# Asking for the modulation's weight blocks four steps ahead, from the point where a group's heads begin

## The chip, the core and the metric

The kernel runs on one core of a Trainium2 chip. The metric is the device time of one execution in microseconds (us); below 0.3% two times of this kernel are taken as no different. TensorE (PE, with its weight loads listed apart as PEld), VectorE (DVE), ScalarE (ACT) and GpSimd (POOL) each run their own instructions in order; almost all transfers between memory and the on-chip buffers are asked for on the queue of SyncE (SP), which also is worked off in order.

## The reference

One layer of a hybrid encoder, for a prompt of 2048 tokens and a sample of 64, width 1024. The part that matters is the modulation, six vectors that depend on the conditioning vectors alone:

```
mod = (c_act @ w_ada + b_ada)[:, None, :]
sh1, sc1, gt1, sh2, sc2, gt2 = jnp.split(mod, 6, -1)
h = rmsnorm(x, g1) * (1 + sc1) + sh1
proj = h @ w_in                                  # pool columns, q, k, v, o, gates
...
mix = jnp.concatenate([pool_out, hs], -1) @ w_out
x = x + gt1 * mix
h2 = rmsnorm(x, g2) * (1 + sc2) + sh2
up = h2 @ w_up
...
x = x + gt2 * ((jax.nn.silu(g) * a) @ w_down)
```

`c_act` has two rows, one for the prompt and one for the sample. `w_ada` is 1024 x 6144 in float32. `sh2`, `sc2` and `gt2` are first needed behind the attention part.

## The kernel before

**Two stages.** The attention stage (input projection, mLSTM heads, pooling, output projection) takes the tokens in four groups of 512, the last with the 64 sample tokens besides. Then the feed-forward stage takes them in three groups of 704. In the trace the attention stage lies between 0 and about 760 us. All matrix products are made of three passes of a high and a low half of each operand; so weights are either split on the chip (ACT makes the high half, L411, DVE the low half, L414) or read back in a form split before.

**One group of the attention stage.** The loop over `groups` (from L1450) first makes the v columns and the gates (`proj_v`, PE at L1133), then for each of four heads three projections (`gemm`, PE at L478) with the mLSTM steps of the head before woven in (`lstm`: the transposes of k at L1298, q by k at L1308, the state update `kw` by `va` at L1323, the read-out at L1343 and L1345), then pooling and the output projection. `lstm`'s vector instructions are recorded by a helper and all stand at L250 in the trace: `kw` is the scaled, transposed k that L1323 needs.

**Work in the background.** Generators lie in the lists `bg`; `tick(i)` moves the first generator of list i one step on. In the second to fourth groups list 3 holds `ada(2 + o.g, False)`, which makes one of `sh2`, `sc2`, `gt2`, and list 4 holds `up_sums` (L852 to L882), which reads `w_up` in pieces into `w4` tiles (L857), forms sums on DVE (L876 to L881) and stores them as `wsum` (L867). Both share SP and DVE with the weights and the mLSTM steps.

**`ada` (L177).** A modulation vector's weights are 16 blocks of 128 x 512 float32, 256 KB each. `load(i)` asks for block i on SP (L194). Step i takes block i and makes two DVE instructions, one for each conditioning row: at L208 for the first block of a half (a product), at L210 for the others (product and sum). In the second to fourth groups `lead` is 3: the first tick asks for blocks 0, 1 and 2, and step i ends with asking for block i + 3.

**Where its ticks are.** In `proj_v` list 3 is ticked for the second product (`hv == 0`) at even token tiles: four times in the second and third groups, six times in the fourth, which has a fifth tile. So the heads begin with step 3, in the fourth group with step 5. After that each `gemm` ticks list 3 twice, once at its fifth weight block and once at its end (L487, L492).

**The tiles.** The blocks lie in `raw` tiles, of which there are five (`RB`, L44). The same five tiles hold the weights that are split on the chip: `w_v` for `proj_v`, and `w_out` for the output projection. The head projections of the second to fourth groups read `hl_kept`, already split, into the seven `wt` tiles (L395) and use no `raw` tile.

**What sets the order.** Only the first group's opening and the feed-forward stage have their instruction order written out by hand (`manual_schedule`, L1457 and L2004). In the rest of the attention stage the framework orders each engine's instructions, SP's requests among them, from the order in which they are written, their dependencies, priorities and free tiles. An instruction can thus stand well ahead of where it is written. Once ordered, the order is fixed, and each engine waits where it must.

## Time and profile before

| | |
|---|---|
| median of 3 runs | 2174.8 us |
| lowest and highest run | 2169.42 us, 2175.45 us |
| the profiled execution's own time | 2174.68 us |
| its span, first to last instruction | 2172.9 us |
| lying around the span | 1.8 us |
| mean granted TensorE clock | 0.998 of full speed |
| requests for blocks of `ada` on SP in the second to fourth groups | 48, of 256 KB each |
| from such a request to its landing, min / median / max | 3.0 / 5.4 / 6.8 us |

The page gives each engine's busy time in the whole span. The views of waits name the instruction that waited, then the one it waited for, then the total in us, the number of times and the longest. The chain of waits follows the work that ended last back to its releasers. A timeline row has start, duration, engine, line, operation and operands, a count, and in brackets the engine's idle time before it with the releaser. A window's row has its length, the busy time of PE, PEld, DVE, ACT and POOL with instruction counts, the granted clock, the DMA share and GB/s.

### The profile page before, as it was taken

How to read it: one execution, taken by the hardware profiler on the slowest of the kernel's cores; microseconds unless marked ns; L12 is line 12 of the kernel's file. 1: busy time of each engine (PE TensorE's matmuls, PEld its weight loads, DVE VectorE, ACT ScalarE, POOL GpSimd, SP SyncE). 2: the span in 40 equal slices, each digit the busy share in tenths (PEclk: the TensorE clock that was granted, in tenths of full speed). 3: DMA queues.
4: the chain of work that ended last, by engine and by line, in shares of the span. 5: the costliest groups of instructions: out<-in, count | busy, mean ns of one | idle time of the engine just before them, and what ended most of it. 6: DMA issues, size and time to landing. Idle time of an engine off the chain costs nothing.

```text
span 2172.9 us, 38060 instructions
## 1 busy us (share of the span) xinstructions
PE 2151.4 (99%) x13553; PEld 2044.4 (94%) x13553; DVE 1634.9 (75%) x3040; ACT 1096.1 (50%) x2181; POOL 258.4 (12%) x475
## 2 busy tenths in 40 slices
PE   8999999999999999999999999999999999999998
PEld 7888888888899999999999999999999999999998
DVE  5878668667955778797967668888886597887874
ACT  4554335334333446464736445655655365565554
POOL 0010000001000201010101220100101321111112
PEclk9999999999999999999999999999999999999999
DMA  8987997987888477888967976666668675555542
GB/s 319 328 305 233 323 321 246 309 302 244 301 283 288 169 260 239 282 292 300 350 214 255 321 245 222 234 208 209 228 222 274 223 255 186 170 177 190 171 160 77
DMA packets 297351, 539.51 MB, mean 248 GB/s; under 512 B 25760, under 2 KB 114336, under 8 KB 297160
## 3 DMA queue, kind: packets, MB, share of 16 engines
q1 hardware_dynamic: 286568, 511.87, 69.6%
q10 hardware_dynamic: 10592, 25.20, 3.0%
q8 instruction: 107, 1.75, 0.3%
q14 instruction: 84, 0.69, 0.1%
HBM read 410.98 MB, written 125.98 MB: 247 GB/s over the span
## 4 chain that ended last, share of the span: by engine, by line
PE 85%; DMA 5%; DVE 5%; issue 2%; ACT 2%; SPq 0%; POOL 0%; DVEq 0%; ACTq 0%; POOLq 0%
PE mm L1594 34%; PE mm L478 22%; PE mm L2160 12%; PE mm L2037 8%; PE mm L1133 3%; DVE wt L414 1%; DMA wt<-wsum 1%; PE m L1323 1%; DMA hl_kept<-wt 1%; PE m L1308 1%; PE m L1343 1%; PE m L1345 1%; DVE tg L1572 1%; DMA raw<-w_qkou 0%; ACT wt L411 0%
## 5 line engine op out<-in xcount | busy, mean ns | idle before, releaser
L1594 PE MATMUL mm<-hx,wt 128*128 128x352 f32 x5544 | 885.9, 321 | 0.7 <-DVE wt L414 0.5
L1594 PEld LDWEIGHTS mm<-hx,wt 128*128 128x128 f32 x5544 | 878.7, 188 | 2.6 <-DVE wt L414 2.0
L478 PE MATMUL mm<-hl,wt 128*128 128x512 f32 (+2 forms) x1920 | 387.4, 357 | 0.0
L411 ACT ACTIVATE wt<-raw 128x512 fp32r<-128x512 f32 (+3 forms) x470 | 276.6, 597 | 177.6 <-PE mm L478 52.8
L478 PEld LDWEIGHTS mm<-hl,wt 128*128 128x128 f32 x1920 | 316.4, 189 | 47.7 <-issue 4.4
L414 DVE TENSOR_TENSOR wt<-raw,wt 128x512 fp32r<-128x512 f32 (+3 forms) x470 | 312.8, 672 | 61.9 <-ACT wt L411 61.7
L2160 PE MATMUL mm<-av,wt 128*128 128x448 f32 (+1 forms) x1632 | 262.7, 322 | 0.0
L2160 PEld LDWEIGHTS mm<-av,wt 128*128 128x128 f32 x1632 | 250.4, 188 | 11.1
L2009 DVE SCALAR_TENSOR_TENSOR x<-mm,MOD,x 128x352 f32<-128x352 f32 (+3 forms) x360 | 167.5, 505 | 77.7 <-PE mm L2160 64.3
L2037 PE MATMUL mm<-av,wt 128*128 128x352 f32 x1344 | 220.7, 323 | 1.9 <-DVE x L2009 0.7
L2037 PEld LDWEIGHTS mm<-av,wt 128*128 128x128 f32 x1344 | 215.4, 188 | 5.0 <-DVE ea L1603 3.0
L1641 ACT ACTIVATE mm<-mm 128x352 f32<-128x352 f32 x196 | 87.8, 448 | 233.7 <-PE mm L1594 177.1
L478 PE MATMUL mm<-mx,wt 128*128 128x512 f32 (+1 forms) x960 | 182.9, 352 | 0.3 <-DVE scr L250 0.3
L478 PEld LDWEIGHTS mm<-mx,wt 128*128 128x128 f32 x960 | 159.4, 188 | 23.0 <-PE mm L478 0.5
L1572 DVE SCALAR_TENSOR_TENSOR ta<-ea,V,ta 128x704 f32<-128x704 f32 (+1 forms) x132 | 125.7, 953 | 58.4 <-ACT ta L1567 54.4
L1572 DVE SCALAR_TENSOR_TENSOR tg<-eg,V,tg 128x704 f32<-128x704 f32 (+1 forms) x132 | 125.7, 952 | 56.8 <-ACT tg L1567 54.3
L414 DVE TENSOR_TENSOR wt<-wt 128x512 fp32r<-128x512 f32 x196 | 133.0, 685 | 12.8 <-ACT wt L411 12.7
L411 ACT ACTIVATE wt<-wt 128x512 fp32r<-128x512 f32 x196 | 119.2, 622 | 36.6 <-DMA wt<-wsum 35.7
L1550 POOL COPY ea<-UC 128x2 f32<-128x2 f32 x66 | 33.1, 501 | 506.2 <-DVE ta L1572 407.3
L1781 ACT ACTIVATE tg<-tg 128x704 f32<-128x704 f32 (+1 forms) x66 | 52.5, 795 | 71.8 <-DVE tg L1572 71.8
L1133 PE MATMUL mm<-wt,hl 128*128 128x256 f32 (+1 forms) x576 | 71.4, 284 | 0.0
L1133 PEld LDWEIGHTS mm<-wt,hl 128*128 128x128 f32 x576 | 70.4, 190 | 0.8 <-issue 0.6
(305 smaller groups left out, 2207.0 us busy)
## 6 DMA issues: line engine op xcount, KB each, us to landing
wt<-wsplit SPq DMA_DIRECT2D x132, 512.0 KB, 4.3
raw<-w_up SPq DMA_DIRECT2D x198, 256.0 KB, 3.8
wt<-hl_kept SPq DMA_DIRECT2D x96, 512.0 KB, 6.3
wt<-wsum SPq DMA_DIRECT2D x132, 256.0 KB, 5.0
wsplit<-wt SPq DMA_DIRECT2D x66, 512.0 KB, 5.1
w<-w_up SPq DMA_DIRECT2D x88, 256.0 KB, 4.4
wsum<-w SPq DMA_DIRECT2D x44, 512.0 KB, 5.9
Bd<-fscr ACTq DMA_DIRECT2D x56, 352.0 KB, 4.3
```

The source lines that it names most:

```text
L411: act.activation(u.w[:, 0, :u.n], u.raw[:, :u.n], AF.Copy)
L414: dve.tensor_tensor(out=u.w[:, 1, :u.n], in0=u.raw[:, :u.n], in1=u.w[:, 0, :u.n].bitcast(F32), op=ALU.subtract)
L478: pe.matmul(ps[bi][:, :hi - lo], U[:, a, k % 4 * P:(k % 4 + 1) * P], mv[k][:, b, lo:hi], start=(at == 0 and pi == 0), stop=(k == order[-1] ...
L1133: pe.matmul(ps[ti][:n, :cols], h[4 * kh + k4][:, b, lo:lo + n], U[:, a, k4 % 2 * cols:(k4 % 2 + 1) * cols], start=(kh == 0 and k4 == 0 and ...
L1550: pool.tensor_copy(ext[:, 0:2], UC[:, f, :])
L1572: dve.scalar_tensor_tensor(out=t[:, :E], in0=ext[:, j:j + E], scalar=wc(j, f), in1=t[:, :E], op0=ALU.mult, op1=ALU.add)
L1594: pe.matmul(bk.t[:, :FH], U[:, a, kc * P:(kc + 1) * P], Bo.at(nm, kc, b), start=(first and kc == 0 and pi == 0), stop=(kc == 3 and pi == 2 ...
L1641: act.activation(to.t[:, :FH], bk.t[:, :FH], AF.Copy)
L1781: act.activation(self.tg[:, :E], self.tg[:, :E], AF.Silu)
L2009: dve.scalar_tensor_tensor(out=x3[n][:, a:b], in0=bk.t[:, a - lo:b - lo], scalar=gt2(n, s), in1=x3[n][:, a:b], op0=ALU.mult, op1=ALU.add)
L2037: pe.matmul(bk.t[:, :FH], U[:, a, c:c + P], quad.put(op, m, b), start=(first and m == 0 and pi == 0), stop=(m == 1 and pi == 2), skip_grou ...
L2160: pe.matmul(bks[i].t[:, :hi - lo], U[:, a, k % 4 * P:(k % 4 + 1) * P], av[k][:, b, lo:hi], start=(k == 0 and (a, b) == PASSES[0]), stop=(k ...
```

## The change

A list `ahead_of_heads` is empty while `proj_v` of the second, third or fourth group is written, and holds an entry from then on. When `ada` ends a step while it holds one and `lead` is still 3, `lead` becomes 4 and one more block is asked for. From there step i asks for block i + 4. No instruction is added: blocks 7 to 15 of the second and third groups and blocks 9 to 15 of the fourth are each asked for one step earlier than before. The first group's `ada` has a `lead` of 4 in both kernels and other tiles, and isn't touched.

```diff
+    ahead_of_heads = []
+
     def ada(m, first):
...
             load(i + lead)
+            if ahead_of_heads and lead == 3:
+                lead = 4
+                load(i + lead)
             yield
         side.append(ada_end(m, accs))
...
             else:
                 cols = []
+                ahead_of_heads.clear()
                 va = proj_v(o, h, cols)
+                ahead_of_heads.append(1)
```

## The prediction

> **What bounds the kernel now.** I read the page's busy times first.

> ```profile
> span 2172.9 us, 38060 instructions
> ...
> PE 2151.4 (99%) x13553; PEld 2044.4 (94%) x13553; DVE 1634.9 (75%) x3040; ACT 1096.1 (50%) x2181; POOL 258.4 (12%) x475
> ```

> PE is idle for 2172.9 - 2151.4 = 21.5 us of the whole span. So I went to the stretches in which the change can act, the four heads of the second, third and fourth groups, in the view by windows (length, then PE's busy time):

> ```profile
> 237.00:347.00 110.00, 110.00 (x581) 92.48 (x581) 77.53 (x173) 40.16 (x113) 9.48 (x13) 1.00 0.84 286
> 415.00:529.00 114.00, 112.15 (x585) 93.89 (x583) 74.67 (x171) 40.65 (x114) 10.21 (x14) 0.99 0.82 279
> 604.00:720.00 116.00, 115.13 (x855) 109.36 (x854) 63.80 (x178) 42.53 (x134) 8.20 (x11) 1.00 0.80 262
> ```

> PE has no gap in the second group, 1.85 us in the third and 0.87 us in the fourth. That is the whole idle time to be won in the place of the change. The view of PE's waits from 405 to 530 us has a single row, which names the third group's gap:

> ```profile
> PE m L1323 <- DVE kw L250: 1.9, 1, 1.9
> ```

> The chain of waits over the same place says why `kw` was late (start, duration, what):

> ```profile
> 427.53 0.63 SPq L194
> ...
> 428.20 5.81 DMA raw<-w_ada
> ```

> A block of `ada`, asked for at 427.53, is 5.81 us on its way; DVE, which works in order, had its update queued ahead of `kw` (DVE's rows stand below), and PE waited for `kw`. This is the event that the change can touch.

> It costs more than its gap. Here is the same run of 39 matmuls, from the first head's L1285 to its read-out, in the second and in the third group, and then the window just behind the gap:

> ```profile
> 255.90:261.80 5.90, 5.90 (x39) 5.17 (x37) 4.28 (x10) 1.14 (x4) 0.00 (x0) 1.00 1.07 392
> 433.70:443.50 9.80, 7.95 (x39) 6.59 (x39) 9.51 (x22) 1.14 (x4) 0.00 (x0) 0.83 0.92 347
> ```

> ```profile
> 438.50:441.90 3.40, 3.40 (x12) 2.94 (x12) 3.29 (x9) 0.00 (x0) 0.00 (x0) 0.50 1.06 407
> ```

> The granted clock is 0.50 for 3.4 us right behind the gap. The PE timeline gives the price exactly:

> ```profile
> 255.75 0.39 PE L1285 MATMUL m<-RHL,E_r 128*128 128x512 f32 x1
> ...
> 261.67 0.39 PE L1343 MATMUL m<-SP,q 128*128 128x129 f32 x2
> ```

> ```profile
> 433.76 0.39 PE L1285 MATMUL m<-RHL,E_r 128*128 128x512 f32 x1
> ...
> 435.24 0.94 PE L478 MATMUL mm<-hl,wt 128*128 128x512 f32 x3
> 438.03 1.65 PE L1323 MATMUL m<-va,kw 128*128 128x129 f32 x8 [1.85 <-DVE kw L250]
> ...
> 443.37 0.38 PE L1343 MATMUL m<-SP,q 128*128 128x129 f32 x2
> ```

> From L1285 to L1343 the second group takes 261.67 - 255.75 = 5.92 us, the third 443.37 - 433.76 = 9.61 us: 3.69 us more, of which 1.85 us is the gap and 1.84 us the slower matmuls (half of 3.4 us would be 1.7 us).

> [...]

> **The change part by part.** *Requests.* None is added and none removed; 9 + 9 + 7 = 25 of the 48 move forward by one step, each past what SP has between two of them. In the third group SP's queue reads:

> ```profile
> 415.29 0.55 SPq L194 DMA_DIRECT2D raw<-w_ada  x1
> 419.25 1.20 SPq L857 DMA_DIRECT2D w<-w_up  x2
> 421.76 0.56 SPq L867 DMA_DIRECT2D wsum<-w  x1
> 422.37 0.62 SPq L194 DMA_DIRECT2D raw<-w_ada  x1
> ...
> 427.53 1.11 SPq L194 DMA_DIRECT2D raw<-w_ada  x2
> ```

> One more pair follows; counted back from the sixteenth, these are blocks 10, 11, and 12 with 13. Between 415.8 and 421.8 SP mostly stands still for `up_sums`, longest for a store that must land before its tile is filled again (the view of the queue's own waits), and the request for block 11 stands behind that:

> ```profile
> SPq L857 <- DMA wsum<-w: 3.3, 1, 3.3
> ```

> Only one or two blocks are on their way, though five `raw` tiles are there. DVE's side:

> ```profile
> 427.40 0.75 DVE L210 SCALAR_TENSOR_TENSOR s<-raw,CA,s 128x512 f32<-128x512 f32 x1 [4.35 <-DMA raw<-w_ada]
> ...
> 433.46 0.75 DVE L210 SCALAR_TENSOR_TENSOR s<-raw,CA,s 128x512 f32<-128x512 f32 x1 [4.49 <-DMA raw<-w_ada]
> ...
> 435.21 0.75 DVE L210 SCALAR_TENSOR_TENSOR s<-raw,CA,s 128x512 f32<-128x512 f32 x1
> ...
> 437.20 0.69 DVE L250 TENSOR_TENSOR kw<-m,CL 128x512 f32<-128x512 f32 x1
> ```

> Steps 11 and 12 wait 4.35 and 4.49 us for their blocks, step 13 for none, and `kw` follows.

> I take it that each moved request gets the place that the request before it has now, and that DVE keeps its order. Then block 11 is asked for at about 415.8, block 12 at 422.4 and block 13 at 427.5. The present request at 427.53 has its block in use at 433.46, 5.9 us later; by that block 11 lands near 421.7, block 12 near 428.3 and block 13 near 433.5. Steps 11 and 12 then have their data some 5 us earlier, and the late one is step 13: it starts at about 433.5 in place of 435.21, 1.7 us earlier, and so does all behind it. `kw` would start at 435.5, end at 436.2, and L1323 could start at 436.3. PE's filling work, the three matmuls at 435.24, ends at 436.18. The gap shrinks from 1.85 to about 0.1 us. With 0.1 us of idling I expect no half clock; that such a gap doesn't bring it can be seen in the fourth group, where 0.87 us in all went with a granted clock of 1.00. Sum: -3.69 + 0.1 = -3.6 us.

> *Bounds of it.* The landings of all 48 requests:

> ```profile
> DMA to landing us min/median/max: 3.0/5.4/6.8
> ```

> If the landing takes 6.8 us, the longest of the 48, block 13 comes 1 us later and the gap is about 1.1 us: with the half clock that is a gain of 0.75 us (1.85 - 1.1), without it of 2.6 us (3.69 - 1.1). If `kw` comes in time altogether, the gain is 3.69 us. Nothing in these windows gives more, but for the 0.87 us of the fourth group; 3.69 + 0.87 = 4.6 us is the upper end.

> *What is pushed back.* A moved request puts what it passes later by its issue (0.55 to 0.62 us) and by its bytes: 262,144 bytes at the 407 GB/s of the window above are 0.64 us. Passed over are `w_up` loads, `wsum` stores and `hl_kept` loads. PE's only wait in 415 to 530 us is that for `kw`, so the weights' cover holds now; without it each would cost up to 0.64 us. I take zero.

> *The tiles.* Four asked ahead and one in use are all five `raw` tiles. A request must now wait for the tile of step i - 1 in place of step i - 2. Where DVE is late, SP waits there with `hl_kept` requests behind it. Bounds: zero where steps are done at once, as in the rows above, where a step's two instructions take 2 x 0.75 us, and one landing, 5.81 us, where a step itself waits for its block; this is SP's time, not PE's, and PE feels it only after the loaded weights run out. I take zero.

> *The other two groups.* A row of DVE in the second group; the last request and the first head's matmuls in the fourth:

> ```profile
> 263.32 0.75 DVE L210 SCALAR_TENSOR_TENSOR s<-raw,CA,s 128x512 f32<-128x512 f32 x1 [2.11 <-DMA raw<-w_ada]
> ```

> ```profile
> 591.42 0.33 SPq L194 DMA_DIRECT2D raw<-w_ada  x1
> ```

> ```profile
> 603.75 14.56 PE L478 MATMUL mm<-hl,wt 128*128 128x256 f32 x108
> ```

> In the second group DVE still waits for a block in the heads, but PE has no gap there (above). In the fourth the sixteenth request goes out 12 us before the heads' first matmul, although the code asks for it in the heads: the ordering has pulled `ada` forward, and one more block asked for in the heads finds nothing to do. Zero for both.

> So the profiled execution would go from 2174.68 to 2171.1 us. That execution lies 0.1 us under the median of the runs; on their scale the forecast is **2171.2 us**, 0.17% less.

> **The rivals.** *The stall stays (2174.8 us).* The order is not the written one: in the fourth group all requests went out before the heads. If free tiles and SP's waits for `up_sums` set the places, asking a step earlier changes nothing, or step 12's wait only passes to step 13 with a longer landing. For it: that wait of 3.3 us on SP, which a request may stay behind. Against it: tiles were free at that time, so it was rank in the queue that held block 11 back.

> *Slower: `ada` gets in front of `kw` in more groups (2182 us).* The place is DVE's queue in the first head of a group. If blocks are asked for earlier, their updates are ordered earlier as well, and an update whose block is late holds back whatever stands behind it. It decides from the point where `kw` is later than the filling matmuls behind L1308. Price from the rows: 3.69 us for a group like the third now; where a 4.49 us wait falls without the 2.64 us that were covered there (4.49 - 1.85), 4.49 + 1.84 = 6.3 us. Hit in the second and fourth groups, with the third as it is: 2174.8 + 2 x 3.69 = 2182.2; at 6.3 us each, 2187. For it: all of DVE's order between 200 and 720 us is open to be made anew, and the 2.11 us wait in the second group needs only to fall a few us earlier. Against it: of three groups one was hit, and earlier requests shorten each wait.

> *More than the stall is won (2167.5 us).* One of the three runs took 2169.42 us, 5.4 us under the median, and no trace shows what it lacked. If it was this event and another like it, 2 x 3.69 = 7.4 us would go. For it: that run. Against: in the windows above no second gap of that kind is seen.

> **How the numbers follow.** I give the forecast 0.47, with a range of its own from 2168.5 to 2174 by its bounds and the runs' scatter. The stall that stays gets 0.25, the slower rival 0.22 and the larger gain 0.06. A measurement of this kernel can't tell 0.3% from no change, that is 6.5 us: faster means under 2168.3, slower over 2181.3. Faster is the larger gain with 0.06 and the lower edge of the forecast with 0.05: 0.11. Slower is what of its rival lies beyond 2181.3, some three quarters, and a little scatter: 0.18. The rest, 0.71, is no change. The range must leave out no more than 2 in 10: 2167.5 to 2182.5 cuts some 0.06 below and 0.14 above.

> **What would show it.** Right: in the third group's SP queue a second request near 415.8; steps 11 and 12 of `ada` without waits of 4 us; no PE wait for `kw` near 438; a granted clock of 1.00 there; L1285 to L1343 in 5.9 us. Wrong: requests in the old places (the stall stays), or new rows of PE waiting for `kw`, `at` or `CL` in the first heads with 3.4 us of half clock behind them (slower). A change in the stretch behind 760 us would be none that I have reckoned with.

## The result, and the profile after

The changed kernel is slower: its median is 2179.28 us (8 runs, 2173.03 to 2182.48) against 2172.78 us for the kernel before, run beside it (8 runs, 2169.42 to 2175.45). The ratio, estimated from all runs, is 1.0026, 95% interval 1.0015 to 1.0036. The forecast was 2171.2 us, 0.17% less. The difference is under the 0.3% below which two times were to count as no different; but the interval leaves out 1, so here, and for the kernels of the experiments, I go by the interval.

The execution that left the profile is the fastest of the eight, 2173.03 us with a span of 2171.2 us. It shows the kind of loss, not its usual size; a profile nearer to the median follows among the experiments. Instructions and bytes are the same as before, and PE's order is the same too, instruction by instruction. DVE's order differs, in two places only: around the first head of the second and of the third group (ACT's differs by one pair, near 446 us). In both, one more step of `ada` stands ahead of `kw` than before: step 12 in the second group, step 14 in the third. Here is the second group's, from CL to `kw` (`ada` stands for one update, the other names for the tile that an instruction writes):

```
before:   CL  RS  GL            kw   at  at  st  ...
after:    CL  RS  GL  ada  ada  kw   at  at  st  ...
```

Line numbers of the changed kernel are up to 7 higher: `kw`, CL and GL are recorded at L255, updates at L212, L1323 is L1328 and so on. The view by windows for the heads of the three groups after (length, PE busy, then the others):

```profile
237.00:347.00 110.00, 109.23 (x576) 91.58 (x575) 75.57 (x171) 39.76 (x113) 9.80 (x13) 1.00 0.85 284
415.00:529.00 114.00, 111.67 (x583) 93.49 (x582) 74.98 (x170) 40.40 (x113) 10.20 (x14) 0.99 0.82 278
```

The second group, which had no gap, has one of 0.77 us; the third group's has grown from 1.85 to 2.33 us. PE's waits after, from 130 to 760 us, name the same culprit for both:

```profile
PE m L1328 <- DVE kw L255: 3.1, 2, 2.3
```

DVE's timeline in the second group after shows how the new gap comes about:

```profile
252.93 0.17 DVE L255 COPY GL<-m 128x16 f32<-128x16 f32 x1 [3.97 <-PE m L1248]
255.93 0.75 DVE L212 SCALAR_TENSOR_TENSOR s<-raw,CA,s 128x512 f32<-128x512 f32 x1 [2.83 <-DMA raw<-w_ada]
256.60 0.74 DVE L212 SCALAR_TENSOR_TENSOR acc<-raw,CA,acc 128x512 f32<-128x512 f32 x1
257.26 0.68 DVE L255 TENSOR_TENSOR kw<-m,CL 128x512 f32<-128x512 f32 x1
```

An update, the first of step 12, now stands ahead of `kw` and waits 2.83 us for its block. In the kernel before the same update stood behind `kw`, where its wait of 2.11 us hurt nobody.

In the third group the requests did move as forecast. SP's queue after:

```profile
415.43 0.73 SPq L196 DMA_DIRECT2D raw<-w_ada  x1
420.36 1.20 SPq L862 DMA_DIRECT2D w<-w_up  x2
421.65 0.55 SPq L196 DMA_DIRECT2D raw<-w_ada  x1
...
427.43 1.40 SPq L862 DMA_DIRECT2D w<-w_up  x2
428.88 1.08 SPq L196 DMA_DIRECT2D raw<-w_ada  x2
```

Counted back from the sixteenth, blocks 11, 12 and 13 are asked for at 415.43, 421.65 and 428.88; the forecast was 415.8, 422.4 and 427.5. But look at what DVE, in its new order, does with them:

```profile
423.20 0.75 DVE L212 SCALAR_TENSOR_TENSOR s<-raw,CA,s 128x512 f32<-128x512 f32 x1
...
425.16 0.75 DVE L212 SCALAR_TENSOR_TENSOR s<-raw,CA,s 128x512 f32<-128x512 f32 x1 [0.55 <-DMA raw<-w_ada]
...
433.61 0.42 DVE L881 TENSOR_TENSOR w<-w 128x256 f32<-128x256 f32 x1 [6.45 <-DMA w<-w_up]
...
436.49 0.75 DVE L212 SCALAR_TENSOR_TENSOR s<-raw,CA,s 128x512 f32<-128x512 f32 x1
...
437.81 0.68 DVE L255 TENSOR_TENSOR kw<-m,CL 128x512 f32<-128x512 f32 x1
```

The rows at 423.20, 425.16 and 436.49 are the first updates of steps 11, 12 and 14. Step 11 waits for nothing and step 12 for 0.55 us, where they waited 4.35 and 4.49 us before: so far the forecast holds. But the next instruction that needs a load, a sum of `up_sums` between steps 12 and 13, now waits 6.45 us for its `w_up`, which was asked for from 427.43 on, in the kernel before from 425.46 on. This wait ends at 433.61, close to the 433.5 at which the forecast had its last late block. What follows is longer than forecast: not only step 13 but also step 14, which started at 440.98 before, behind `kw`, and the fourth of the sums stand ahead of `kw`. From the end of the wait to `kw` it takes 437.81 - 433.61 = 4.20 us, where the forecast counted 435.5 - 433.5 = 2.0 us. So `kw` starts 0.6 us later than before.

### The profile page after: what moved, and what is told of

Its sections match the earlier page's. It is cut to its first block, busy times and chain, and to the rows that moved or that the text cites. A ratio compares the mean times of both kernels' runs of the same rounds, so it can differ in the third digit from the quotient of the medians.

```text
span 2171.2 us, 38057 instructions
## 1 busy us (share of the span) xinstructions
PE 2150.0 (99%) x13553; PEld 2044.2 (94%) x13553; DVE 1634.0 (75%) x3040; ACT 1094.3 (50%) x2181; POOL 260.3 (12%) x475
## 4 chain that ended last, share of the span: by engine, by line
PE 86%; DVE 5%; DMA 5%; issue 2%; ACT 1%; POOL 0%; SPq 0%; ACTq 0%; POOLq 0%; DVEq 0%
PE mm L1601 36%; PE mm L483 21%; PE mm L2167 12%; PE mm L2044 8%; PE mm L1138 3%; DVE wt L419 1%; DMA hl_kept<-wt 1%; PE m L1328 1%; DMA w<-w_up 1%; PE m L1313 1%; DMA wsum<-w 1%; PE m L1348 1%; PE m L1350 1%; DMA wt<-wsum 1%; DVE tg L1579 1%
```

## The experiments

Theory A: the loss comes from DVE's order around the first head's `kw`. Rival B: from the transfers, which asking earlier pushes back. Rival C: from chance at the start and the end of the run. Rival D, added later: from the work of the updates themselves.

**One group at a time.** Only the second group asks four steps ahead:

```diff
-                ahead_of_heads.append(1)
+                if o.g == 1:
+                    ahead_of_heads.append(1)
```

> Blocks are asked for four steps ahead in the second group alone; the third and fourth keep three. In the order of DVE's queue the first head of the second group then has one step of the modulation (two updates) between GL and kw, which the kernel before has behind kw; the third group's queue is as before. PE's order is the same in all of these kernels. Theory A (DVE's order): the loss sits in the second group's first head, where kw waits behind an update whose block is late. This kernel should lose nearly all that the change lost: 4 to 7 us over the kernel before (ratio 1.002 to 1.003), and its profile should show PE waiting for kw near 258 us. Rival B (the transfers: blocks asked for earlier push back weights, sums and stores): about half of the loss, 2 to 3 us, with no wait of PE for kw there. Rival C (the two kernels differ only by how the clock's windows fall at the start and the end): no difference beyond 1 us.

Measured: median 2177.76 us (11 runs) against 2174.52, ratio 1.0013 (1.0004 to 1.0021); the kernel before had 35 runs beside these experiments. PE's timeline in its profile has the gap in the second group, with the third's still there:

```profile
260.93 1.13 PE L1328 MATMUL m<-va,kw 128*128 128x129 f32 x8 [2.26 <-DVE kw L255]
```

```profile
441.84 2.06 PE L1328 MATMUL m<-va,kw 128*128 128x129 f32 x8 [2.67 <-DVE kw L255]
```

The same edit with `o.g == 2` is the third group alone:

> Four steps ahead in the third group alone. Its first head has three steps of the modulation or parts of them in front of kw, as before; what changes is that steps 11 and 12 are earlier and that a sum of up_sums with a late w_up stands ahead of them. Theory A: within 2 us of the kernel before, since kw is late in both (1.85 us of PE waiting before, 2.3 us in the profile of the changed kernel). Rival B: 2 to 3 us slower. The forecast's step (the third group's stall goes): 3 us faster.

Measured: 2174.92 us (11 runs) against 2174.52, ratio 1.0002 (0.9994 to 1.0011). The gap in its profile:

```profile
440.01 1.13 PE L1328 MATMUL m<-va,kw 128*128 128x129 f32 x8 [3.26 <-DVE kw L255]
```

So the loss sits in the second group, though with 3.2 us it is under the 4 us that A gave as a lower end. In the third group one late wait took the place of another and nothing was won. The two ratios split unevenly, as A says; by B both groups would have paid. Their intervals overlap, so the stronger evidence is PE's wait for `kw` in the second group, which B had excluded.

**`kw` ahead of the updates.** The updates that are written behind the first head's `kw` are queued behind it on DVE in the second and third groups (this sets the order of issue and makes no wait). Only the steps up to 8 are left ahead of that `kw`, where the kernel before had those up to 11 and up to 13; in the third group the sums of `up_sums` go behind `kw` with the updates:

```diff
+            with tc.issue_after(first_kw[-1]) if first_kw else nullcontext():
                 for s in range(2):
...
+                if hd == 0 and o.g in (1, 2):
+                    first_kw.append(made.ins)        # made: the instruction that writes kw
```

First with three steps ahead throughout, then on the changed kernel:

> The kernel before (three steps ahead), with the updates of the steps that are written behind the first head's kw also queued behind it on DVE, in the second and third groups. No instruction is added; DVE's queue then has CL, RS, GL, kw without an update between them. Theory A: PE's wait for kw near 438 us goes, and the half clock behind it: 2 to 5 us faster than the kernel before (3.69 us from the profile). Rival B and C: no difference beyond 1 us, the wait being a matter of transfers or chance. Point at which A fails: kw still late in the profile, or a wait for at or st in its place, since the updates now stand behind kw and ahead of at and st.

> The changed kernel (four steps ahead in all three groups) with the same updates queued behind the first head's kw. DVE's queue around the first heads is that of the kernel before with the same addition; the requests on SP are those of four steps ahead. Theory A: the requests themselves cost nothing, so this is within 1 us of the kernel before with that addition, that is 2 to 5 us faster than the kernel before and 7 to 10 us faster than the changed kernel. Rival B: the loss of 5 to 6 us against three steps ahead stays.

Measured: 2171.12 us (12 runs) against 2174.52 for three steps, ratio 0.9984 (0.9975 to 0.9992); 2172.55 us (11 runs) for four, ratio 0.9986 (0.9977 to 0.9994). In the three-step kernel's profile DVE's rows around GL in the second group, and the windows over the first head in the second and third groups, are:

```profile
252.93 0.17 DVE L253 COPY GL<-m 128x16 f32<-128x16 f32 x1 [4.78 <-PE m L1246]
255.84 0.69 DVE L253 TENSOR_TENSOR kw<-m,CL 128x512 f32<-128x512 f32 x1 [2.73 <-PE m L1301]
```

```profile
253.50:263.50 10.00, 10.00 (x63) 8.86 (x62) 7.41 (x17) 2.93 (x11) 0.00 (x0) 1.00 1.06 379
431.50:446.00 14.50, 14.50 (x83) 12.54 (x82) 11.00 (x27) 6.24 (x21) 1.45 (x1) 1.00 1.03 370
```

`kw` now waits for nothing but PE's own transposes, PE has no gap and the clock stays at 1.00. Both kernels are faster than the one before, by 0.16% and 0.14%. Against the changed kernel the four-step one gains 5 to 7 us by the medians, where A gave 7 to 10.

A also said that four steps and three would be within 1 us of each other once the order is held. By the ratios they are 0.4 us apart, by the medians 1.4 us, and intervals of some 1.8 us to each side can't decide that. The profiles can, for these stretches: PE's, DVE's and ACT's orders are the same in the two kernels and only SP's differs, PE waits for nothing between 200 and 620 us in either, and the first heads take 5.92 us in both (table at the end of this section). That is against B: here the requests and their transfers cost PE nothing. The loss is in the order that they bring along. Whether an update or a sum of `up_sums` holds `kw` in the third group isn't separated by this edit, since both went behind it.

**The changed kernel again, and the two groups crossed with the order.** `first_kw` is filled in one group only, on the changed kernel (`o.g == 1`, then `o.g == 2`).

> The changed kernel once more, for a profile of an execution nearer to its median (the one shown is the fastest of its eight) and for a ratio on the same chip as the next three. Theory A: 1.0015 to 1.003 of the kernel before; PE waits for kw in the first head of the second and of the third group, each with half clock behind it where the gap is long enough. Rival C: a profile at its median shows no more waiting in 200 to 620 us than the kernel before, and the difference lies outside.

> The changed kernel, with the updates queued behind the first head's kw in the second group alone. Theory A: the second group's loss goes and the third's stall stays, as in the kernel before: within 1.5 us of the kernel before. Rival B (requests asked for earlier cost by themselves): 3 us or more slower than the kernel before.

> The changed kernel, with the updates queued behind the first head's kw in the third group alone. Theory A: the second group's new stall stays and the third's goes: each is worth 2.5 to 3.7 us by the earlier runs, so within 2 us of the kernel before. Together with the one above: the two groups' effects add up, so that the changed kernel is as far above these two as these are above the one with both.

The changed kernel's second measurement gave 2177.64 us (9 runs) against 2174.64, ratio 1.0017 (1.0007 to 1.0027). The profiled execution has a span of 2175.9 us. PE's timeline in the second and third groups, then DVE's in the second:

```profile
262.16 2.06 PE L1328 MATMUL m<-va,kw 128*128 128x129 f32 x8 [2.81 <-DVE kw L255]
```

```profile
444.59 1.13 PE L1328 MATMUL m<-va,kw 128*128 128x129 f32 x8 [2.73 <-DVE kw L255]
```

```profile
254.96 0.17 DVE L255 COPY GL<-m 128x16 f32<-128x16 f32 x1 [3.54 <-PE m L1248]
260.00 0.75 DVE L212 SCALAR_TENSOR_TENSOR s<-raw,CA,s 128x512 f32<-128x512 f32 x1 [4.87 <-DMA raw<-w_ada]
260.67 0.75 DVE L212 SCALAR_TENSOR_TENSOR acc<-raw,CA,acc 128x512 f32<-128x512 f32 x1
261.33 0.68 DVE L255 TENSOR_TENSOR kw<-m,CL 128x512 f32<-128x512 f32 x1
```

Here the update waits 4.87 us, not 2.83, and the gap is 2.81 us, not 0.77. The block's landing differs from execution to execution, and the gap with it: the update starts 7.3 us after its block was asked for (252.69), in the first profile 5.3 us (250.62). That is part of why the fast execution shown first had so little of the loss: of the 4.7 us between the two spans the gaps make 5.5 - 3.1 = 2.4 us, and the rest lies outside these heads. The two gaps are 5.5 us together against 1.85 us in the kernel before, with one stretch of half clock (3.41 us at 0.50) in each kernel: 3.7 us more, as much as the ratio (0.17% of 2174.64 is 3.7 us).

With the second group's order held: 2173.74 us (11 runs), ratio 1.0000 (0.9991 to 1.0009). With the third's: 2175.48 us (11 runs), ratio 1.0007 (0.9998 to 1.0016). Each has the other group's gap, in the profiles 1.96 us and 2.52 us:

```profile
438.24 1.13 PE L1333 MATMUL m<-va,kw 128*128 128x129 f32 x8 [1.96 <-DVE kw L258]
```

```profile
261.82 2.06 PE L1333 MATMUL m<-va,kw 128*128 128x129 f32 x8 [2.52 <-DVE kw L258]
```

In ratios, the changed kernel stands at 1.0017, with the second held 1.0000, with the third held 1.0007, with both 0.9986 (this one measured among the earlier experiments): holding the second is worth 0.17% and 0.21%, holding the third 0.10% and 0.14%. They add up within their intervals.

**The updates' work without their wait.** Three steps ahead and both orders held, with two instructions of an update's size between GL (`gl_made` holds the instructions that write it) and `kw`:

```diff
+            if hd == 0 and o.g in (1, 2):
+                with tc.issue_after(gl_made[-1]):
+                    for _ in range(2):
+                        dve.scalar_tensor_tensor(out=kw[:, 0:4, :].rearrange("p a t -> p (a t)"), in0=q[:, :GT], scalar=1.0,
+                                                 in1=q[:, :GT], op0=ALU.mult, op1=ALU.add)
```

> Three steps ahead and the updates queued behind the first head's kw in the second and third groups; added between GL and kw in these two groups are two DVE instructions of the size of an update, which read the first head's q (long there) and write into kw's tile ahead of the real kw. They wait for no block. Theory A (it is the late block that an update waits for, not the update's own time on DVE): no wait of PE for kw, and the time of the kernel without the added two within 1 us, that is 2 to 5 us faster than the kernel before. Rival D (the updates' 1.4 us of work in front of kw is what makes it late): PE waits for kw in both groups, and the time is that of the changed kernel or at least that of the kernel before.

Measured: 2170.64 us (11 runs) against 2174.64, ratio 0.9985 (0.9976 to 0.9994), as good as 0.9984 without the added two. DVE's rows in the second group:

```profile
254.09 0.17 DVE L253 COPY GL<-m 128x16 f32<-128x16 f32 x1 [4.77 <-PE m L1246]
254.18 1.41 DVE L253 SCALAR_TENSOR_TENSOR kw<-q 128x512 f32<-128x512 f32 x2
256.99 0.69 DVE L253 TENSOR_TENSOR kw<-m,CL 128x512 f32<-128x512 f32 x1 [1.40 <-PE m L1307]
```

The 1.41 us of work end 1.40 us before PE's transposes let `kw` start, and in the third group `kw` waits the same 1.40 us for PE. Rival D falls: two updates fit in front of `kw`. It is the late load ahead of `kw` that does the harm, with whatever is queued between the two.

**One measure for all profiles.** PE's order is the same, record by record, in all ten profiles of this case. So the prediction's own measure, the time from the first head's L1285 to its read-out at L1343 (start to start, in us), can be read in each. The last column is the measured ratio's difference from 1, taken of 2174.6 us:

| kernel | second group | third group | both, less the kernel before | by the ratio |
|---|---|---|---|---|
| before | 5.92 | 9.61 | | |
| changed, first profile (its fastest run) | 6.89 | 10.07 | +1.4 | +5.7 |
| changed, second profile | 10.42 | 8.87 | +3.8 | +3.7 |
| four steps in the second group alone | 8.41 | 10.24 | +3.1 | +2.8 |
| four steps in the third group alone | 5.92 | 10.98 | +1.4 | +0.4 |
| three steps, both orders held | 5.92 | 5.93 | -3.7 | -3.5 |
| four steps, both orders held | 5.92 | 5.92 | -3.7 | -3.0 |
| four steps, second group's order held | 5.93 | 9.70 | +0.1 | 0.0 |
| four steps, third group's order held | 10.14 | 5.92 | +0.5 | +1.5 |
| three steps, both held, work added | 5.90 | 5.93 | -3.7 | -3.3 |

But for the first profile, the two heads account for each kernel's difference to about 1 us. That is against C, by which the difference would lie outside them.

## Why the prediction was wrong

*What bounds the kernel, and the event to be touched.* Right. The chain from a late block by DVE's order to `kw` and PE was the one that mattered, and its removal was worth about what was said: 3.6 us were forecast, and the kernel with the order held is 2174.52 - 2171.12 = 3.4 us faster by the medians; its third group's first head takes 5.93 us in place of 9.61.

*The requests.* Right in the third group, to within 1.4 us for each of the three. But of the 25 that were to move only seven passed another transfer on SP: blocks 12 and 14 in the second group, 8, 10, 11, 12 and 14 in the third. In the fourth none did, as forecast.

*"DVE keeps its order."* This is the step that failed. Only the requests were moved in the program, and DVE's order was made anew as well: one more step of `ada` came ahead of `kw` in each of the two groups. In the third group the waits of steps 11 and 12 went as forecast, but a late `w_up` ended at the same time as the forecast's late block, and behind it step 14 and a fourth sum now stood ahead of `kw`: 4.20 us of work in place of 2.0. The gap that was to shrink from 1.85 to 0.1 us was 2.33 and 2.73 us in the two profiles, so the gain of 3.6 us didn't come. In the second group, which I had priced at zero because DVE waited there and PE didn't, step 12 moved from behind `kw` to ahead of it, and its late block held PE: the first head took 6.89 and 10.42 us in place of 5.92, a loss of 1.0 and 4.5 us where the sum had none. The row that I quoted there, a wait of 2.11 us shortly behind `kw`, was the warning.

*The half clock as part of a gap's price.* Too simple. It was right for the gap of 1.85 us before, whose removal gave back 9.61 - 5.93 = 3.68 us. But by the table's measure the gaps of 2.26 and 2.73 us cost 2.49 and 2.95 us, little more than themselves; the last section has what the traces show of it.

*The rivals.* The slower rival had the mechanism, `ada` in front of `kw`, and the place, the first heads. It hit one more group and not two; by its own price for one, 3.69 us, it would have given 2178.5 us, against 2179.28 and 2177.64 measured. Its chance of 0.22 was too low against 0.47 for a forecast that needed an order made anew to stay as it was. The stall that stays was right for the third group. The larger gain was not seen; the run of 2169.42 us behind it is within the scatter of the kernel before.

*Pushed-back transfers, the five tiles, the fourth group.* Priced at zero for PE, and the kernel with four steps and the order held bears that out in the two first heads; in the fourth group PE's and DVE's orders are unchanged. For DVE the price wasn't nothing: in the changed kernel's third group a load of `w_up` that was asked for later became the late one.

## What to carry to other kernels

A request moved in a program that is ordered by machine can move its consumers too. Before pricing an earlier load, ask where the instruction that waits for it will stand on an in-order engine (DVE here: `kw` started only behind an update that had waited 2.83 us), and what that engine's next urgent instruction is; compare the two orders before trusting any old timeline. If a background update can be late, queue it explicitly behind the urgent instruction: here that edge was worth 0.14 to 0.16%, while the step from three to four without it lost time, and with it made no difference that these runs could tell.

## What the runs showed of the hardware

The traces' records of the clock show more. In the kernel before the clock is at full from 8.40 us, where its records begin, at half from 438.48 us for 3.413 us, and at half again from 2165.62 us. In the changed kernel's first profile these times are 9.41, 439.49 (again for 3.413 us) and 2166.64 us. In both, 430.08 us lie between the first and the second of them, 126 times 3.4133 us, and 2157.22 us between the first and the third, 632 times. In two more profiles I count steps of that length from the one half clock that each has in these heads. In the changed kernel's second profile the half clock begins at 261.82, and counted on by 53 steps another step begins at 442.72. Here are windows of one step each: for each gap the step that holds most of it, and the next (PE's busy time is the second number, the granted clock the last but two):

```profile
258.41:261.82 3.41, 0.94 (x6) 0.46 (x4) 1.82 (x3) 0.10 (x1) 0.00 (x0) 1.00 1.06 392
261.82:265.23 3.41, 3.07 (x11) 2.89 (x12) 2.88 (x8) 0.00 (x0) 0.00 (x0) 0.50 1.05 389
...
442.72:446.14 3.42, 1.55 (x11) 1.50 (x12) 3.32 (x7) 0.00 (x0) 0.00 (x0) 1.00 1.07 403
446.14:449.55 3.41, 3.41 (x23) 2.99 (x22) 3.12 (x9) 0.28 (x1) 0.00 (x0) 1.00 0.95 352
```

The first gap has 3.41 - 0.94 = 2.47 us within one step, and half clock followed. The second is cut at 442.72 into 0.87 and 1.87 us, and none followed. With the second group alone four steps ahead it was the other way round: the second group's gap of 2.26 us has 1.86 us in one step and no half clock behind it, the third's of 2.67 us has 2.27 us in one step, and the half clock begins with the next, while PE still waits:

```profile
257.12:260.54 3.42, 1.55 (x11) 1.07 (x9) 1.77 (x3) 0.70 (x3) 0.00 (x0) 1.00 1.04 384
260.54:263.95 3.41, 3.02 (x17) 2.69 (x18) 3.20 (x9) 0.00 (x0) 0.00 (x0) 1.00 1.03 388
...
438.03:441.44 3.41, 1.14 (x7) 0.66 (x6) 3.41 (x8) 0.29 (x2) 0.00 (x0) 1.00 1.07 393
441.44:444.86 3.42, 3.02 (x11) 2.86 (x12) 3.23 (x9) 0.00 (x0) 0.00 (x0) 0.50 1.05 407
```

The profiles hold ten waits of PE for `kw`. Seven have half clock behind them. Four of these can be placed in steps: 1.85 us of idling within one step in the kernel before (435.07 to 438.48), 2.33 us in the changed kernel's first profile (436.08 to 439.49), and the 2.47 and 2.27 us above. The other three are the gaps of 3.26, 1.96 and 2.52 us among the experiments, with a granted clock of 0.88, 0.88 and 0.90 in the windows over those heads (431.5 to 446 us for the first two, 253.5 to 263.5 us for the third). The three waits without half clock have 0.77 us (255.17 to 258.58 in the changed kernel's first profile), 1.86 and 1.87 us within one step. So between 1.85 and 1.87 us both were seen. By the table's measure the seven cost 1.65 to 1.84 us more than their length, the three 0.20 to 0.23 us more. At the end of the span, among the last matmuls, half clock came after steps with 1.90 us of idling in the kernel before (2162.21 to 2165.62) and 2.08 us in the changed kernel's first profile (2163.22 to 2166.64). All this is read off afterwards: no run moved a gap on purpose, and none shows a limit from which half clock begins.
